# Norm's root and reciprocal on partitions, and one plain tile fewer in each feed-forward of a hybrid layer

## The chip, the cores and the metric

The kernel runs on 1 core of one Trainium2 chip. The metric is the device time of one execution in microseconds (us). A core has TensorE (PE, with its weight loads shown apart as PEld), VectorE (DVE), ScalarE (ACT), GpSimd (POOL) and SyncE (SP, which here only issues DMAs). Each engine takes its own instructions in order.

## The reference, cut to what matters

One transformer layer over 512 tokens with width 1024, all in fp32, with a feed-forward at either end:

```python
h = h + 0.5 * swiglu(rmsnorm(h, ffn1_norm), ffn1_w1, ffn1_w3, ffn1_w2)    # feed-forward a, D_FF = 2816
u = rmsnorm(h, mix_norm)
z = u @ w_in                       # q, k, v, gates of two attentions (NSA and MoBA)
h = h + (sigmoid(gate_a) * y_nsa + sigmoid(gate_b) * y_moba) @ w_out
h = h + 0.5 * swiglu(rmsnorm(h, ffn2_norm), ffn2_w1, ffn2_w3, ffn2_w2)    # feed-forward b
h = h + sigmoid(rmsnorm(h, ple_norm) @ w_ple_gate) * (p @ w_ple)
out = rmsnorm(h, final_norm)
# rmsnorm(x, g) = x * rsqrt(mean(x*x) + 1e-6) * g ;  swiglu = (silu(x@w1) * (x@w3)) @ w2
```

The row factor `rsqrt(...)` of a norm belongs to a token, so it can be multiplied in after a product with a weight matrix. The change concerns the row factors of three norms (those before feed-forward a, before the mixing stage, and before feed-forward b) and the two feed-forwards.

## The kernel before

Activations stand transposed: features on the 128 partitions, the 512 tokens in the free dimension. Each fp32 operand of a product is split in a high and a low part of a faster type, and a product is three matmuls, high by high, high by low, low by high (`mm3`, L226 to L229). A weight unit of 128x1024 arrives by DMA (`raw`), its high part is made on ACT (L76, in places POOL), its low part on DVE (L77); both stand in `whl`, of which there are three buffers.

**The norm's row factor.** `norm_rows` (L215) is called three times: for "a" and "b" inside `ffn_seven`, for "m" at L833, ahead of the mixing stage. `ssum` holds the squares summed over the 8 feature tiles. One fp32 matmul with a matrix of ones (L218) sums over the partitions and leaves each token's sum on all 128 partitions; ACT takes the root of the 128x512 (L220), DVE its reciprocal (L221). The result `R` has each token's factor on every partition. The norm ahead of the last stage (L1079 to L1084) is done in another way already: four matmuls with the tokens as output partitions and two columns of ones, a root and a reciprocal of 128x8.

**The feed-forward** (`ffn_seven`, L236) works through 22 tiles of 128 hidden features. The first `PLAIN` of them (6 in a, 5 in b) are *plain* tiles (L416 to L438): 24 matmuls of 512 columns for w1, 24 for w3. Their results are scaled by `R` and gated in `gate` (L253): two multiplications by `R`, one product, one low part on DVE; a silu and a high part on ACT. The others are *seven* tiles (L446 to L502): a tile's w1 and w3 are cut in quarters so that seven half-size products do for eight, 84 matmuls of 256 columns (`prod`, L346). These need other operands, the *forms*: `normal` (L295) multiplies `h` by gain and `R`, 8 instructions on DVE; `forms` (L298), 4 calls, makes sums and differences and splits them, 8 DVE and 4 ACT instructions each. Normals and forms are queued in `todo` and handed out one entry for each plain tile once `R` exists (L432). So the plain tiles are the time in which `R`, the normals, the forms and the first seven tile's weights (`wa`, `s2h`, `wb`) get ready. From the last plain tile on, each tile's result `gf` stays in fp32 until `convert` (L371) splits it at the end of the tiles; feature tile d of the down projection (L515 to L523) then runs over all 22 tiles in order.

**Order of the work.** Outside `tc.manual_schedule()` blocks a planner orders each engine's instructions ahead of time: earlier in the source means more urgent, but an instruction whose inputs the planner does not expect to be ready yet is passed by a later one. Inside those blocks (the seven tiles and the converts) the order is the source's. `tc.issue_after` keeps `norm_rows` in a feed-forward behind the w1 matmuls. PSUM has 8 banks by tag: "mm" 2, "s" 3, "t" 2, "po" 1. `p1` of a plain tile takes an "mm" bank, so tile f + 2 waits for `gate` of tile f. The sum `nb` takes a "t" bank, and so does the product `vcmp` right behind the norm "m" (L834).

Of the kernel before, what the change touches and what calls it, by code (L numbers as in the profile page):

```python
# [8 lines left out]
F32 = mybir.dt.float32  # L9
F32R = mybir.dt.float32r  # L10
AF = mybir.ActivationFunctionType
# [4 lines left out]
P = 128  # L16
S = 512
D = 1024
# [3 lines left out]
BIG = 1e30  # L22
EPS = 1e-6
NC_BLK = 31
PLAIN = {"a": 6, "b": 5}


class Weights:
# [87 lines left out]
def tile_hybrid_layer(ctx: ExitStack, tc: tile.TileContext, io, out):  # L116
    nc = tc.nc
    PSUM = bass.MemoryType.PSUM
    act, dve, pool, pe = nc.scalar, nc.vector, nc.gpsimd, nc.tensor

    def sbuf(stack, name, bufs=1):
        return stack.enter_context(tc.tile_pool(name=name, bufs=bufs, reuse_waits="tile"))
# [4 lines left out]
    nrm = sbuf(ctx, "nrm", 2)  # L127
# [4 lines left out]
    def bank(tag, name):  # L132
        return ps.tile([P, 512], F32, tag=tag, name=name, bufs={"s": 3, "po": 1}.get(tag, 2))
# [3 lines left out]
    for f in range(NF):  # L137
        units += [(("w1a", f), io["w1a"][f])]
        if f < PLAIN["a"]:
            units += [(("w3a", f), io["w3a"][f])]  # L140
# [17 lines left out]
    for f in range(NF):  # L158
        units += [(("w1b", f), io["w1b"][f])]
        if f < PLAIN["b"]:  # L160
            units += [(("w3b", f), io["w3b"][f])]
# [24 lines left out]
    ident = cst.tile([P, P], F32, name="ident")  # L186
    make_identity(nc, ident)
    ones = cst.tile([P, P], F32, name="ones")
    pool.memset(ones, 1.0)
    eps = cst.tile([P, 1], F32, name="eps")  # L190
# [3 lines left out]
    ssum, last_part = [None], [None]  # L194
# [20 lines left out]
    def norm_rows(n):  # L215

        b = bank("t", f"nb{n}")
        pe.matmul(b, lhsT=ones, rhs=ssum[0], start=True, stop=True)  # L218
        r = nrm.tile([P, S], F32, tag="R", bufs=1, name=f"R{n}")
        act.activation(r, b, AF.Sqrt, bias=eps, scale=1.0 / D)  # L220
        dve.reciprocal(r, r)  # L221
        return r

    last_mm = [None]
# [1 line left out]
    def mm3(out_ap, w, ah, al, first, last):  # L226
        pe.matmul(out_ap, lhsT=w[:, 0], rhs=ah, start=first, stop=False)  # L227
        pe.matmul(out_ap, lhsT=w[:, 0], rhs=al, start=False, stop=False)  # L228
        last_mm[0] = pe.matmul(out_ap, lhsT=w[:, 1], rhs=ah, start=False, stop=last)  # L229
# [5 lines left out]

    def ffn_seven(sfx, n, PLAIN, again, first=None):  # L236

# [15 lines left out]
        def gate(f, b1, b3):  # L253
            t1 = tp.tile([P, S], F32, tag="t1", name=f"t1{sfx}{f}")
            dve.tensor_mul(t1, b1, R)
            act.activation(t1, t1, AF.Silu)
            if f < PLAIN - 1:
                t3 = tp.tile([P, S], F32, tag="t3", name=f"t3{sfx}{f}")
            else:
                t3 = gf[f] = home(f)  # L260
            dve.tensor_mul(t3, b3, R)
            dve.tensor_mul(t3, t3, t1)
            if f < PLAIN - 1:
                ghl[f] = gp.tile([P, 2, S], F32R, tag=f"g{f}", name=f"g{sfx}{f}")
                parts(ghl[f], t3)

        def home(f):

            j = f - (PLAIN - 1)
            if j < 2 * KD:  # L270
# [24 lines left out]
        def normal(d):  # L295
            dve.scalar_tensor_tensor(h[d], h[d], gain[:, n - 1, d:d + 1], R, op0=ALU.mult, op1=ALU.mult)

        def forms(k):  # L298
            if not f11:
                form_tiles()  # L300
            a, b = h[k], h[k + 4]
            parts(f11[k], a[:, lo_])
            parts(f2[k], b)
            dve.tensor_sub(a[:, lo_], a[:, lo_], a[:, hi_])
            dve.tensor_sub(a[:, hi_], a[:, hi_], b[:, hi_])
            dve.scalar_tensor_tensor(b[:, hi_], a[:, lo_], -1.0, b[:, hi_], op0=ALU.mult, op1=ALU.subtract)
            dve.tensor_add(b[:, lo_], b[:, lo_], b[:, hi_])
            parts(f13[k], a)
            parts(f42[k], b)
# [4 lines left out]
        def load_sums(f):  # L314
            if f >= NF:
                return
            t = sums[f] = sp.tile([P, 2, Q], F32, tag="s13", name=f"s13{f}")
            nc.sync.dma_start(t[:, 0], w1[f][:, 0:Q])
            nc.sync.dma_start(t[:, 1], w3[f][:, Q:D])
            pool.dma_start(t, w3[f][:, 0:Q].unsqueeze(1).to_broadcast([P, 2, Q]), accum_op=ALU.add)  # L320

        def load_last(f):
            if f >= NF:
                return
            t = raws[f] = sp.tile([P, 2, Q], F32, tag="lr", name=f"lr{f}")
            nc.sync.dma_start(t[:, 1], w3[f][:, Q:D])
# [54 lines left out]
        def up_first(b1, b3):  # L381

            ws = [fp.tile([P, 2, 1024], F32R, tag=t, name=f"whl{u}") for u, t in enumerate(("fa", "fb0"))]
            odd = sp.tile([P, S], F32, tag="s2h", name="odd")
            ssum[0] = nrm.tile([P, S], F32, tag="ssum", bufs=1, name="ssum0")
            sqs = []
            with tc.manual_schedule():
                for k in range(KD):
                    if k % 2 == 0:
                        W.split_piece(0, k * P, k * P + 256, ws[0])  # L390
                    scaled(k, first, False)
                    if k % 2 == 0:
                        W.split_piece(1, k * P, k * P + 256, ws[1])
                    c = slice(k * P, (k + 1) * P)
                    for b, w in zip((b1, b3), ws):
                        mm3(b, w[:, :, c], uh[k], ul[k], k == 0, k == KD - 1)
                    if k % 2 == 0:
                        sq2 = sp.tile([P, 2, S], F32, tag=("s13", "lr")[k // 4], name=f"sq0_{k}")
                    act.activation(sq2[:, k % 2], h[k], AF.Square)
                    sqs.append(sq2[:, k % 2])  # L400
                    if k == 5:
                        pool.tensor_add(odd, sqs[1], sqs[3])
                act.activation(dummy, eps, AF.Sqrt)
                pool.tensor_add(odd, odd, sqs[5])
                pool.tensor_add(odd, odd, sqs[7])
                W.skip(2)
                for k in range(2, KD, 2):
                    dve.tensor_add(ssum[0], sqs[0] if k == 2 else ssum[0], sqs[k])
                W._split()
                dve.tensor_add(ssum[0], ssum[0], odd)  # L410
# [3 lines left out]
        todo = [lambda d=d: normal(d) for d in (0, 4, 1, 5, 2, 6, 3, 7)], *([lambda k=k: forms(k)] for k in range(4))  # L414
        todo = list(todo)
        for f in range(PLAIN):  # L416
            b1, b3 = bank("mm", f"p1{sfx}{f}"), bank("s", f"p3{sfx}{f}")
            if first is not None and f == 0:
                up_first(b1, b3)
            else:  # L420
                for b, key in ((b1, "w1"), (b3, "w3")):
                    w = W.get((key + sfx, f))
                    for k in range(KD):
                        c = slice(k * P, (k + 1) * P)
                        mm3(b, w[:, :, c], uh[k], ul[k], k == 0, k == KD - 1)
                    if R is None:
                        with tc.issue_after(last_mm[0].ins):
                            R = norm_rows(sfx)
            if last is not None:
                gate(*last)  # L430
            last = (f, b1, b3)
            if R is not None and todo:  # L432
                for x in todo.pop(0):
                    x()
            if f == PLAIN - 2:
                for x in range(2):
                    load_sums(PLAIN + x)
                    load_last(PLAIN + x)  # L438
# [76 lines left out]
        for d in range(KD):  # L515
            b = bank("t", f"p2{sfx}{d}")
# [7 lines left out]
        st.close()  # L524

    ffn_seven("a", 1, PLAIN["a"], io["xT"], 0)


# [100 lines left out]
    bias = [hp.tile([P, 4, 4, 32], F32, tag=f"h{6 + g}", name=f"bc{g}") for g in range(2)]  # L629
# [374 lines left out]
    def up_tile(w, e, o0, name):  # L1004
        b = bank("s" if o0 else "t", name)
        for k in range(4):
            c = slice((e * 4 + k) * P, (e * 4 + k + 1) * P)
            mm3(b, w[:, :, c], oh[o0 + k], ol[o0 + k], k == 0, k == 3)
        return b

    for d2 in range(4):
# [5 lines left out]
        for e in range(2):  # L1017
            d = 2 * d2 + e
            b = up_tile(w, e, 0, f"yn{d}")
            dve.tensor_mul(ga[d], b, ga[d])  # L1020
        w = W.get(("um", d2))
        for e in range(2):
            d = 2 * d2 + e
            b = up_tile(w, e, 4, f"ym{d}")
            t = gbq[d]
# [8 lines left out]
    for d in range(KD):  # L1034
        w = W.get(("wo", d))
        b = bank("mm", f"wo{d}")
        for k in range(KD):
            c = slice(k * P, (k + 1) * P)
# [29 lines left out]
    for i in range(4):  # L1068
        t = slice(i * P, (i + 1) * P)
        for e in range(2):  # L1070
            c = slice(e * 512, e * 512 + 512)
            b = bank("mm" if e else "s", f"pl{i}{e}")
# [12 lines left out]
    for i in range(4):  # L1085
        for e in range(2):
            b = bank("t" if e else "po", f"ht{i}{e}")
# [5 lines left out]
    for i in range(4):  # L1093
        t = slice(i * P, (i + 1) * P)
        ss, r = fin[:, i, 6:7], fin[:, i, 7:8]
        parts = [(0, 512), (512, 1024)] if i < 3 else [(0, 512), (512, 768), (768, 1024)]
        for e, (c0, c1) in enumerate(parts):
            c, n = slice(c0, c1), c1 - c0
            b = bank("mm" if e % 2 else "s", f"pg{i}{e}")[:, :n]
# [82 lines left out]
```

## Time and profile before

| | |
|---|---|
| median of 3 runs | 1193.08 us (1192.45 to 1193.95) |
| the profiled execution: time, span of its instructions | 1193.96 us, 1192.2 us |
| granted TensorE clock over the span | 0.999 of 2.4 GHz |
| PE busy | 1172.8 us (98%), 6714 matmuls |
| PEld busy | 1020.3 us (86%) |
| DVE busy | 796.3 us (67%) |
| ACT busy | 547.8 us (46%) |
| POOL busy | 192.9 us (16%) |

The span runs from the first to the last instruction; 1.8 us of the execution lie around it. Matmuls are pipelined: a row's own duration contains the flow through the array, so the cost of one matmul in a stream is the distance from its start to the next one's start.

### The profile page before, as it was taken

How to read it: one execution, taken by the hardware profiler on the slowest of the kernel's cores; microseconds unless marked ns; L12 is line 12 of the kernel's file. 1: busy time of each engine (PE TensorE's matmuls, PEld its weight loads, DVE VectorE, ACT ScalarE, POOL GpSimd, SP SyncE). 2: the span in 40 equal slices, each digit the busy share in tenths (PEclk: the TensorE clock that was granted, in tenths of full speed). 3: DMA queues.
4: the chain of work that ended last, by engine and by line, in shares of the span. 5: the costliest groups of instructions: out<-in, count | busy, mean ns of one | idle time of the engine just before them, and what ended most of it. 6: DMA issues, size and time to landing. Idle time of an engine off the chain costs nothing.

```text
span 1192.2 us, 17522 instructions
## 1 busy us (share of the span) xinstructions
PE 1172.8 (98%) x6714; PEld 1020.3 (86%) x6714; DVE 796.3 (67%) x1304; ACT 547.8 (46%) x920; POOL 192.9 (16%) x261
## 2 busy tenths in 40 slices
PE   8999999999999999999999999999999999999997
PEld 5889999988887878888888888888999999888876
DVE  6987777763336787776776655578777777533454
ACT  5544444542224564554457223354444445322355
POOL 3001111010025244333432100000111110100000
PEclk9999999999999999999999999999999999999999
DMA  7537777353333521212221343463677772533411
GB/s 240 156 90 187 185 179 185 102 197 113 116 109 110 164 71 36 72 36 78 82 89 54 124 137 124 140 182 106 151 182 177 191 183 80 183 97 97 155 56 53
DMA packets 57459, 151.09 MB, mean 127 GB/s; under 512 B 6256, under 2 KB 7408, under 8 KB 57376
## 3 DMA queue, kind: packets, MB, share of 16 engines
q1 hardware_dynamic: 41616, 116.77, 30.5%
q0 software_dynamic: 11584, 25.86, 11.4%
q10 hardware_dynamic: 4176, 7.36, 1.7%
q8 instruction: 52, 0.85, 0.3%
q14 instruction: 31, 0.25, 0.1%
HBM read 140.53 MB, written 6.29 MB: 123 GB/s over the span
## 4 chain that ended last, share of the span: by engine, by line
PE 87%; DVE 5%; issue 3%; POOL 2%; ACT 1%; DMA 1%; SPq 0%; ACTq 0%; POOLq 0%; DVEq 0%
PE pbb L351 6%; PE pba L351 6%; PE pab L351 4%; PE pdb L351 4%; PE paa L351 4%; PE pda L351 4%; PE p2b L227 3%; PE p2a L228 3%; PE p2a L229 3%; PE p2b L228 3%; PE p2b L229 3%; PE p2a L227 3%; DVE whl L77 2%; PE wo L228 1%; PE wo L227 1%
## 5 line engine op out<-in xcount | busy, mean ns | idle before, releaser
L77 DVE TENSOR_TENSOR whl<-raw,whl 128x1024 fp32r<-128x1024 f32 (+2 forms) x137 | 163.7, 1198 | 137.8 <-ACT whl L76 128.4
L76 ACT ACTIVATE whl<-raw 128x1024 fp32r<-128x1024 f32 (+2 forms) x105 | 106.5, 1019 | 238.2 <-issue 72.6
L341 DVE TENSOR_TENSOR wa<-raw,wa 128x1024 fp32r<-128x1024 f32 x33 | 40.4, 1225 | 63.1 <-ACT wa L338 63.1
L320 POOL DMA_DIRECT2D s<-in_w3b x17 | 20.6, 1210 | 254.3 <-DVE ssum L213 75.2
L74 POOL TENSOR_SCALAR whl<-raw 128x1024 fp32r<-128x1024 f32 x32 | 35.6, 1112 | 110.6 <-PE gb L229 29.8
L320 POOL DMA_DIRECT2D s<-in_w3a x16 | 19.5, 1218 | 177.7 <-DVE s L330 64.8
L341 DVE TENSOR_TENSOR wl<-lr,wl 128x1024 fp32r<-128x1024 f32 x33 | 40.1, 1216 | 4.1 <-ACT wl L338 4.1
L338 ACT ACTIVATE wb<-s 128x1024 fp32r<-128x1024 f32 x33 | 35.0, 1060 | 13.1 <-PE pbb L351 5.7
L341 DVE TENSOR_TENSOR wb<-s,wb 128x1024 fp32r<-128x1024 f32 x33 | 40.2, 1218 | 0.0
L362 ACT ACTIVATE c<-c 128x256 f32<-128x256 f32 x33 | 13.8, 418 | 57.4 <-DVE c L361 57.4
L228 PE MATMUL m<-ul,whl 128*128 128x512 f32 x96 | 37.8, 393 | 0.0
L229 PE MATMUL m<-uh,whl 128*128 128x512 f32 x96 | 37.7, 393 | 0.0
L227 PE MATMUL m<-uh,whl 128*128 128x512 f32 x96 | 37.6, 391 | 0.0
L338 ACT ACTIVATE wl<-lr 128x1024 fp32r<-128x1024 f32 x33 | 35.0, 1060 | 3.7
L338 ACT ACTIVATE wa<-raw 128x1024 fp32r<-128x1024 f32 x33 | 34.7, 1052 | 0.2 <-PE p3a L229 0.2
L351 PE MATMUL pbb<-fd,s2h 128*128 128x256 f32 x204 | 27.5, 284 | 0.2 <-DVE s2h L334 0.2
L351 PE MATMUL pab<-fc,wa 128*128 128x256 f32 x204 | 27.4, 284 | 0.0
L351 PE MATMUL pbb<-fc,wl 128*128 128x256 f32 x204 | 27.3, 283 | 0.0
L351 PE MATMUL pdb<-fd,wl 128*128 128x256 f32 x204 | 27.3, 283 | 0.0
L351 PE MATMUL pdb<-fb,wb 128*128 128x256 f32 x204 | 27.3, 283 | 0.0
L351 PE MATMUL pbb<-fb,wb 128*128 128x256 f32 x204 | 27.3, 283 | 0.0
L351 PE MATMUL pab<-f,wa 128*128 128x256 f32 x204 | 27.3, 283 | 0.0
(968 smaller groups left out, 3568.0 us busy)
## 6 DMA issues: line engine op xcount, KB each, us to landing
raw<-in_win SPq DMA_DIRECT2D x38, 512.0 KB, 3.7
raw<-in_w1b SPq DMA_DIRECT2D x22, 512.0 KB, 4.7
raw<-in_w1a SPq DMA_DIRECT2D x21, 512.0 KB, 4.8
s<-in_w3b POOLq DMA_DIRECT2D x17, 512.0 KB, 5.7
s<-in_w3a POOLq DMA_DIRECT2D x16, 512.0 KB, 5.8
raw<-in_w2a SPq DMA_DIRECT2D x16, 512.0 KB, 3.5
raw<-in_w2b SPq DMA_DIRECT2D x16, 512.0 KB, 3.6
s<-in_w1b SPq DMA_DIRECT2D x17, 256.0 KB, 3.2
```

The costliest lines, as they stand in the source:

```text
L74: nc.gpsimd.tensor_scalar(hi, src, 1.0, 0.0, op0=ALU.mult, op1=ALU.add)
L76: nc.scalar.activation(hi, src, AF.Copy)
L77: nc.vector.tensor_sub(lo, src, hi.bitcast(F32))
L227: pe.matmul(out_ap, lhsT=w[:, 0], rhs=ah, start=first, stop=False)
L228: pe.matmul(out_ap, lhsT=w[:, 0], rhs=al, start=False, stop=False)
L229: last_mm[0] = pe.matmul(out_ap, lhsT=w[:, 1], rhs=ah, start=False, stop=last)
L320: pool.dma_start(t, w3[f][:, 0:Q].unsqueeze(1).to_broadcast([P, 2, Q]), accum_op=ALU.add)
L338: act.activation(t[:, 0], src, AF.Copy)
L341: dve.tensor_sub(t[:, 1], src, t[:, 0].bitcast(F32))
L351: pe.matmul(b, lhsT=w[:, wz, c], rhs=fm(k, z), start=(first and k == 0 and wz + z == 0), stop=(k == 3 and wz == 1), skip_group_check=not f ...
L362: act.activation(c1[f][:, hi_], c1[f][:, hi_], AF.Silu)
```

## The change

`norm_rows` sums with the tokens on output partitions, as the last norm does: four fp32 matmuls with `ssum` as weights and two columns of ones. Root and reciprocal are taken of 128x8. Four TensorE transposes of a broadcast column spread the factors over the partitions again, into a second "t" bank, and ACT copies them to `R`. `PLAIN` falls from 6 to 5 and from 5 to 4, so 17 and 18 tiles are seven tiles instead of 16 and 17. The first plain tile after `R` takes two entries of `todo`, the normals and the first forms, so that all are still handed out.

```diff
-PLAIN = {"a": 6, "b": 5}
+PLAIN = {"a": 5, "b": 4}
...
     def norm_rows(n):

         b = bank("t", f"nb{n}")
-        pe.matmul(b, lhsT=ones, rhs=ssum[0], start=True, stop=True)
+        for i in range(4):
+            pe.matmul(b[:, 2 * i:2 * i + 2], lhsT=ssum[0][:, i * P:(i + 1) * P], rhs=ones[:, 0:2], start=True, stop=True)
+        c = nrm.tile([P, 8], F32, tag="rc", bufs=1, name=f"rc{n}")
+        act.activation(c, b[:, 0:8], AF.Sqrt, bias=eps, scale=1.0 / D)
+        dve.reciprocal(c, c)
+        rb = bank("t", f"rb{n}")
+        for i in range(4):
+            pe.transpose(rb[:, i * P:(i + 1) * P], c[:, 2 * i:2 * i + 1].to_broadcast([P, P]), ident)
         r = nrm.tile([P, S], F32, tag="R", bufs=1, name=f"R{n}")
-        act.activation(r, b, AF.Sqrt, bias=eps, scale=1.0 / D)
-        dve.reciprocal(r, r)
+        act.activation(r, rb, AF.Copy)
         return r
...
-            if R is not None and todo:
+            while R is not None and len(todo) >= PLAIN - f:
                 for x in todo.pop(0):
                     x()
```

## Rows read from the trace of the kernel before

**Rows 1.** The page's first part: busy time of each engine, its share of the span, and instructions.

```profile
PE 1172.8 (98%) x6714; PEld 1020.3 (86%) x6714; DVE 796.3 (67%) x1304; ACT 547.8 (46%) x920; POOL 192.9 (16%) x261
```

**Rows 2.** Busy time of each engine in stretches of the span: the plain tiles of a after its row factor, and the start of the mixing stage. Columns: stretch, its length, then busy us (instructions) of PE, PEld, DVE, ACT, POOL; granted clock, DMA share, GB/s.

```profile
42.00:76.00 34.00, 34.00 (x152) 28.17 (x151) 33.13 (x59) 16.75 (x24) 0.00 (x0) 1.00 0.35 107
372.00:388.00 16.00, 14.54 (x70) 11.40 (x69) 9.58 (x10) 6.86 (x9) 15.11 (x15) 1.00 0.32 96
```

**Rows 3.** What PE waited for, over the whole span: us in total, times, longest.

```profile
PE vB L227 <- DVE n01l L786: 1.6, 1, 1.6
```

**Rows 4.** PE in order of time, the first w1 matmul of the plain tiles 3 and 4 of a. Columns: start, us, engine, line, output and inputs, shapes, count.

```profile
43.78 0.39 PE L227 MATMUL p1a<-uh,whl 128*128 128x512 f32 x1
...
54.66 0.39 PE L227 MATMUL p1a<-uh,whl 128*128 128x512 f32 x1
```

**Rows 5.** PE in order of time, the first product of the seven tiles 6, 8 and 21 of a (12 matmuls each), and the second product of the first seven tile of b.

```profile
76.42 1.60 PE L351 MATMUL paa<-f,wa 128*128 128x256 f32 x12
...
94.36 1.60 PE L351 MATMUL paa<-f,wa 128*128 128x256 f32 x12
...
225.40 1.60 PE L351 MATMUL paa<-f,wa 128*128 128x256 f32 x12
...
833.29 1.60 PE L351 MATMUL pbb<-fd,s2h 128*128 128x256 f32 x12
```

**Rows 6.** PE in order of time, the norm's sum over the partitions in a (with the second matmul behind it), m and b.

```profile
26.39 1.02 PE L218 MATMUL nba<-ssum,ones 128*128 128x512 f32 x2
...
27.48 0.40 PE L228 MATMUL p3a<-ul,whl 128*128 128x512 f32 x1
...
363.51 1.02 PE L218 MATMUL nbm<-ssum,ones 128*128 128x512 f32 x2
...
782.00 1.02 PE L218 MATMUL nbb<-ssum,ones 128*128 128x512 f32 x2
```

**Rows 7.** PE in order of time, the last stage: the sum of the last norm (L1081), transposes (L1089) and the gate's matmuls (L1102 to L1104). In the source all transposes stand ahead of the gate's matmuls.

```profile
1134.51 0.95 PE L1081 MATMUL nbl<-ones,ssum 128*128 128x2 f32 x8
1135.32 1.07 PE L1089 MATMUL ht<-ident,hq 128*128 128x128 f32 x8
1136.14 0.48 PE L1102 MATMUL pg<-whl,uh 128*128 128x512 f32 x1
...
1138.43 0.66 PE L1089 MATMUL ht<-ident,hq 128*128 128x128 f32 x4 [1.57 <-DVE hn L1090]
1138.84 0.47 PE L1104 MATMUL pg<-whl,ul 128*128 128x512 f32 x1
1139.15 0.40 PE L1102 MATMUL pg<-whl,uh 128*128 128x512 f32 x1
```

**Rows 8.** Single instructions by line (duration in ns, min/median/max; first and last start): the root and the reciprocal of 128x8 and the table loads ahead of the roots of m and b; then, from ACT in order of time, a copy of 128x512 out of PSUM.

```profile
L1083 ACT ACTIVATE rn<-nbl,eps x1: 267/267/267, 1138.3 to 1138.3; 128x8 f32<-128x8 f32 x1
L1084 DVE RECIPROCAL rn<-rn x1: 193/193/193, 1139.7 to 1139.7; 128x8 f32<-128x8 f32 x1
L220 ACT ACT_TABLE_LOAD  x2: 1283/1283/1283, 364.8 to 783.3; - x2
1138.46 0.58 ACT L1090 COPY hn<-ht 128x512 f32<-128x512 f32 x1
```

**Rows 9.** ACT and DVE in order of time: root and reciprocal of a, and the first instruction that uses the row factor in a, m and b.

```profile
27.55 0.67 ACT L220 ACTIVATE Ra<-nba,eps 128x512 f32<-128x512 f32 x1
28.82 3.35 DVE L221 RECIPROCAL Ra<-Ra 128x512 f32<-128x512 f32 x1
32.20 0.69 DVE L255 TENSOR_TENSOR t1a<-p1a,Ra 128x512 f32<-128x512 f32 x1
...
370.24 0.69 DVE L644 TENSOR_TENSOR cf<-kcmp,Rm 128x512 f32<-128x512 f32 x1
...
788.67 5.39 DVE L296 SCALAR_TENSOR_TENSOR hr<-hr,gain,Rb 128x512 f32<-128x512 f32 x8
```

**Rows 10.** DVE in order of time, in the plain tiles of a and b: two low parts of weights, the first multiplication of the gate of tile 1, and the low parts of the first seven tile's weights.

```profile
39.91 2.35 DVE L77 TENSOR_TENSOR whl<-raw,whl 128x1024 fp32r<-128x1024 f32 x2
42.19 0.68 DVE L255 TENSOR_TENSOR t1a<-p1a,Ra 128x512 f32<-128x512 f32 x1
...
73.62 0.68 DVE L334 TENSOR_TENSOR s2h<-s,s2h 128x512 fp32r<-128x512 f32 x1
74.22 1.22 DVE L341 TENSOR_TENSOR wb<-s,wb 128x1024 fp32r<-128x1024 f32 x1
...
827.88 0.68 DVE L334 TENSOR_TENSOR s2h<-s,s2h 128x512 fp32r<-128x512 f32 x1
```

**Rows 11.** The down projection of b: its first matmul and the low-part matmul of tile 13 on PE, and the converts of tiles 13 to 16 on DVE.

```profile
1003.88 0.40 PE L227 MATMUL p2b<-gb,whl 128*128 128x512 f32 x1
...
1012.98 0.42 PE L228 MATMUL p2b<-gbfc,whl 128*128 128x512 f32 x1
...
1012.15 2.50 DVE L251 TENSOR_TENSOR gbfc<-gfb,gbfc 128x512 fp32r<-128x512 f32 x4
```

**Rows 12.** The start of the mixing stage: POOL's sums for the compression inputs, the scaling of the second query tile on DVE, and the matmul that waits for its bank on PE.

```profile
371.01 16.93 POOL L653 TENSOR_TENSOR xa<-cf,pos 64x248 f32<-64x248 f32 x16 [4.78 <-DVE cf L644]
386.78 0.68 DVE L559 SCALAR_TENSOR_TENSOR q1f<-q,Rm 128x512 f32<-128x512 f32 x1
387.60 0.47 PE L227 MATMUL kA<-uh,whl 128*128 128x512 f32 x1 [1.46 <-DVE q1f L559]
```

## The prediction

> **What bounds the kernel now.** I read the page's busy times first: PE is busy for 98% of the span, DVE for 67% [rows 1], so the time is PE's instruction stream and the few places where that stream stops. Then the list of PE's waits, which is short; the one that lies behind the norms and could move is 1.6 us for `vB` [rows 3], and a second one shows in PE's order of time, 1.46 us ahead of `kA` [rows 12]. Last the stretches: in the plain tiles of a PE never stops, but DVE is busy for 33.1 of 34.0 us beside it [rows 2]. So PE is the bound and DVE is just below it there. A change can gain by making PE's stream shorter or by removing a wait; a plain tile dropped takes 10.9 us of cover away from DVE.
>
> **The tile that changes its kind.** A plain tile lasts 54.66 - 43.78 = 10.88 us on PE, 48 matmuls at 0.227 us [rows 4]. Thirteen seven tiles last 225.40 - 94.36 = 131.04 us, 10.08 us each, 84 matmuls at 0.120 us [rows 5]. One tile in each feed-forward: 2 x (10.08 - 10.88) = **-1.60 us**.
>
> The Trainium skill (TensorE: Matmul & The Clock Gate, section Back-to-back issue gap) puts the gap between matmuls at the columns over 2.4 GHz plus 2.5 ns, so 216 ns and 109 ns here; a plain tile would take 10.4 us, a seven tile 9.2 us, and the term would be -2.4 us. Both distances in this trace are longer (227 and 120 ns), the short one by more, so the sum keeps the rows' -1.60.
>
> **The norm on PE, three times.** Before: the sum starts at 26.39, the second matmul behind it at 27.48, so the first would start at 27.25 in a plain stream: 0.86 us [rows 6]. After: eight passes of the two-column form, 1135.32 - 1134.51 = 0.81 us; four transposes, 1138.84 - 1138.43 = 0.41 us; and after each block the next 512-column matmul costs about 0.09 more than 0.227 (behind the transposes 1139.15 - 1138.84 = 0.31) [rows 7]. That is 0.81 + 0.41 + 2 x 0.09 = 1.40, or +0.54 each, **+1.62 us** for three. So on PE alone the two halves of the change cancel. The stationary operand is a broadcast column, which no row shows; it has 128 columns as the shown transposes have, so I take their price.
>
> **When R is there.** Removed from the chain: a root of 128x512 and a reciprocal of 3.35 us on DVE [rows 9]. Added: root 0.27, reciprocal 0.19, copy 0.58 [rows 8], transposes 0.66 to their end [rows 7], and two more handovers between engines, estimated at 0.1 each. In m and b the chain behind the table load goes from 0.69 + 3.35 to 1.90 us: R comes about 2.1 us earlier, near 368.1 instead of 370.24 and near 786.6 instead of 788.67 [rows 9]. The table load of 1.28 us stays in both [rows 8]. In a the reciprocal could start at 28.82 as now, since DVE is in a low part until then; 3.35 - 0.19 - 0.66 - 0.58 - 0.3 leaves 1.6 us, so the first use moves from 32.20 to about 30.6.
>
> **Whether DVE still finishes in time.** Between the first use of R and the low part of `s2h`, DVE works without a gap. One tile fewer removes four gate instructions at a distance of 0.60 and two low parts of weights at 1.14 (42.19 - 39.91 is 2.28 for two) [rows 10]: 4.68 us. In a `s2h` is ready at 74.22 now, then at 74.22 - 1.6 - 4.68 = 67.9. PE needs it in the third matmul of the second product: first seven tile at 76.42 - 10.88 + 0.54 = 66.1, one product of 1.44 and two matmuls later, 67.8 [rows 5, 10]. That is 0.2 us late. The second place is the gate of tile 1, which frees the bank for `p1` of tile 3: the first forms now stand ahead of it, five half-size and three full-size DVE instructions, estimated from the 0.60 at 3.5 us. So it ends at 42.19 - 1.6 + 3.5 + 0.7 = 44.8 against a need at 43.78 + 0.54 = 44.3 [rows 4, 10]. Late by 0.5; what PE waits here it need not wait at `s2h`, so a costs **+0.5 us** (bounds: 0, if the planner puts the gate first, and 1.6, if none of R's gain reaches DVE). In b `s2h` moves from 828.5 to 828.5 - 2.1 - 4.68 = 821.7 and is needed at 833.29 - 10.88 + 0.54 + 0.24 = 823.2 [rows 5, 10]: 1.5 us to spare, nothing.
>
> **The down projection.** It runs over the tiles in order, 0.68 us each, while the converts are still being made in a written order. In b the first convert of the group that starts at 1012.15 ends near 1012.84, and PE's low-part matmul of tile 13 starts at 1012.98, so 0.14 us is to spare [rows 11]. With one tile more to convert, the same place in that order holds tile 12, needed 0.68 earlier: **+0.54 us** in b. In a the order comes to stand as it stands in b now, where PE does not stop: nothing.
>
> **The mixing stage.** Ahead of `kA` PE waits 1.46 us for a bank that `q1f` empties at 386.78, after a chain that starts with POOL's 17 us of sums behind R [rows 12]. All of it moves 2.1 us earlier, while PE is 0.54 later, so the wait goes: **-1.46 us**. Bounds: 0, if DVE's order puts other work ahead of `q1f`; no more than 1.46.
>
> **Waits that the change adds.** The transposes wait for root and reciprocal, and behind them in PE's queue stand the matmuls of the same tile. The last stage shows that the planner lets later matmuls pass transposes that are not ready: the source has all transposes first, but gate matmuls run at 1136.14 and 1138.84 between them [rows 7]. It shows too that it can be wrong by 1.57 us. Bounds: 0, and the whole chain, worked out below as a rival. Between them I take 0.1 each, **+0.3 us**. Each added seven tile brings its own loads, one of them issued and summed through POOL's queue, in place of a plain tile's two; POOL is busy for 16% [rows 1] and the order of the loads stays. ACT gets a copy of 0.58 for a root of 0.67. Nothing for these.
>
> **The sum:** -1.60 + 1.62 + 0.5 + 0.54 - 1.46 + 0.3 = -0.1 us. It is made against the profiled execution's 1193.96 us (span 1192.2 and 1.8 around it), which lies 0.9 above the median of 1193.08. On the median: **1193.0 us**.
>
> **The rivals.**
> *The transposes stop PE (slower).* If the planner puts them right behind the sum, PE waits for the whole chain. The sum ends 0.95 after its start; in m at 364.5, in b at 783.0 [rows 6, 7], table load, root and reciprocal end near 366.7 and 785.1 [rows 8]: 2.2 us each; in a about 1.8. Together 6.2 instead of 0.3: 1198.9 us. In m the bank of `vcmp` does the same, if both "t" banks are given to the norm first. It decides from 2.8 us in all three. The mixed order in rows 7 speaks against, the 1.57 us there for. Chance 0.14.
> *Every cover holds and the wait at `vB` goes too (faster).* -1.60 + 1.62 - 1.46 - 1.63 = -3.1: 1190.0 us. The planner orders the attention anew, and R's users lie ahead of that wait; but its releaser is a small DVE instruction far from R [rows 3]. Chance 0.14.
> *R comes no earlier*, because splits of weights go ahead of the chain on ACT and DVE, while 10.9 us of cover are gone: a is then late by 1.8 and b by 0.6 instead of 0.5 and 0: 1194.9 us, with `kA`'s wait back 1196.3. That would be the change not doing what it says. In a, ACT takes the root 0.2 after the sum [rows 6, 9], so little stands ahead of it. Chance 0.07.
> *`kA` still waits* because DVE's order keeps `q1f` late: 1194.5 us. Chance 0.12.
> *The transposes run one after the other*, each for the 0.27 us of its row and not for the distance of 0.10: 4 x 0.27 - 0.41 = 0.67 more in each norm, 1195.0 us. Four in 0.66 us to the last one's end speak against it [rows 7]. Chance 0.04. The Trainium skill (TensorE: Matmul & The Clock Gate, section Part 4: PE-mode transpose) gives about 275 ns for a transpose within a kernel; by that rule this rival would be the forecast. The trace agrees with the duration, not with a stream of that distance.
>
> **How the numbers follow.** The forecast as summed has 0.49; its own range is the new plan's chance of shifting waits by about 1.4 us either way, 1191.6 to 1194.4. The 8-in-10 range goes on toward the faster rival and over the last three: 1190.5 to 1195.8; outside it stay most of the first two rivals' far ends. A measurement of this kernel can tell about 0.2% (2.4 us) from no change. Faster than 1190.7: the faster rival and 0.01, 0.15. Slower than 1195.5: the first rival and about half of the third, 0.17. The rest, 0.68, is within.
>
> **What would show each step.** In the trace after: a seven tile still 10.08 apart; about 1.4 us of PE per norm; first uses of R near 30.6, 368, 786.5; no wait at `kA`; a wait of about 0.5 at `p1a` of tile 3 or `s2h`; about 0.5 in the down projection of b behind a `gbfc` convert; none there in a. The prediction is wrong if the transposes show waits of 1 us or more, if DVE is over 1 us late at the first seven tile, or if the attention's waits, re-planned, change by more than 2 us in sum.

## The result, and the profile after

| | us, median (lowest to highest, runs) | profiled execution | span | mean granted clock |
|---|---|---|---|---|
| before | 1193.20 (1192.45 to 1193.95, 4) | 1193.96 | 1192.2 | 0.999 |
| after | 1200.26 (1199.78 to 1201.27, 4) | 1200.47 | 1198.8 | 0.998 |

The ratio is 1.0058, with a 95% interval of 1.0046 to 1.0069: slower by 7 us, where 1193.0 was forecast and 1195.8 was the upper end. Of one kernel below (128 bytes and `h6`) two slow executions, 1275.53 and 2341.08 us, are left out of its median. First the busy times of the changed kernel, to be read against [rows 1]:

```profile
PE 1181.1 (99%) x6816; PEld 1025.8 (86%) x6816; DVE 794.7 (66%) x1318; ACT 554.1 (46%) x931; POOL 195.2 (16%) x263
```

PE has 102 instructions more, as the change has it: 10 in each of three norms (eight passes and four transposes for two passes) and 36 in each of two tiles (84 matmuls for 48). But it is busy for 8.3 us more, and the sum priced these 102 at 0.02 us. Then PE's waits over the whole span (us in total, times, longest):

```profile
PE p1a L234 <- DVE ul L202: 2.1, 3, 1.4
PE vB L233 <- DVE n01l L792: 1.6, 1, 1.6
PE pba L357 <- ACT s2h L338: 1.4, 1, 1.4
...
PE pba L357 <- DVE s2h L340: 0.9, 2, 0.6
...
PE p2b L234 <- DVE gbfc L257: 0.3, 1, 0.3
```

The wait of `kA` [rows 12] is gone, the one of `vB` [rows 3] is as it was, and feed-forward a has new ones, for `s2h`, of 2.1 us at its first seven tile. So one part of the loss is a wait, and a larger part lies in time in which PE counts as busy. Where, one sees by cutting the span at the first instruction of each stage, by PE's order of time. The last column is a repaired kernel that the experiments below lead to. (The first row, the start, differs by a us between executions that do the same work there: it is 25.69 in the kernel with all moved by 32 bytes and 26.64 in the one with 512 unused bytes.)

| from the first instruction of ... to that of ... | before | after | difference | repaired |
|---|---|---|---|---|
| start to `nba` | 26.39 | 27.21 | +0.82 | 25.79 |
| `nba` to `paa` (plain tiles of a) | 50.03 | 40.51 | -9.52 | 39.53 |
| `paa` to `p2a` (seven tiles of a) | 161.93 | 174.68 | +12.75 | 172.09 |
| `p2a` to `kcmp` (down projection) | 119.71 | 119.74 | +0.03 | 119.74 |
| `kcmp` to `nbm` | 5.45 | 5.60 | +0.15 | 5.45 |
| `nbm` to `kA` | 24.09 | 23.38 | -0.71 | 23.04 |
| `kA` to `yn` | 266.62 | 267.84 | +1.22 | 266.75 |
| `yn` to `p1b` | 122.31 | 123.17 | +0.86 | 122.30 |
| `p1b` to `nbb` | 5.47 | 5.59 | +0.12 | 5.46 |
| `nbb` to `pab` (plain tiles of b) | 49.86 | 40.51 | -9.35 | 39.51 |
| `pab` to `p2b` (seven tiles of b) | 172.02 | 182.04 | +10.02 | 182.04 |
| `p2b` to `nbl` | 130.63 | 131.36 | +0.73 | 131.31 |
| `nbl` to the end | 57.69 | 57.17 | -0.52 | 56.19 |

Two things are out of line. The seven tiles of a grow by 12.75 us, where those of b grow by 10.02, one tile. And stretches that the change does not touch are longer by small amounts. The shortest of these is the plainest: 24 matmuls of 512 columns, from the first of `p1b` to the sum of the norm, with no wait between them. The view is PE in order of time; first the kernel before, whose sum starts at 782.00 [rows 6], then the changed one.

```profile
776.53 0.39 PE L227 MATMUL p1b<-uh,whl 128*128 128x512 f32 x1
```

```profile
782.13 0.40 PE L233 MATMUL p1b<-uh,whl 128*128 128x512 f32 x1
...
787.72 0.95 PE L219 MATMUL nbb<-ones,ssum 128*128 128x2 f32 x8
```

5.47 / 24 = 0.228 us before, 5.59 / 24 = 0.233 after: the same matmul on the same operands, with a longer step from one start to the next. Over the whole trace (mean step between neighbouring starts within one tile, worked out from the start times, without steps over 1.2 times the median) it is so wherever `uh`, `ul` meet the split weights `whl`: `kcmp` 226.7 to 233.3 ns, the last gate `pg` 226.9 to 233.4, the gates `gb` 228.1 to 233.0. The output logits `pl` keep 226.6 and 226.8, the down projections 226.7 to 227.0; the up projections and `wo` have 233.2 to 233.5 in both. Each difference of means times its count is in sum some 6.7 us.

The second thing, in a: PE around its first seven tile, and beside it DVE.

```profile
67.72 1.60 PE L357 MATMUL paa<-f,wa 128*128 128x256 f32 x12
70.74 0.51 PE L357 MATMUL pba<-fd,s2h 128*128 128x256 f32 x2 [1.43 <-ACT s2h L338]
71.88 1.46 PE L357 MATMUL pba<-fd,s2h 128*128 128x256 f32 x10 [0.64 <-DVE s2h L340]
...
68.14 0.68 DVE L257 TENSOR_TENSOR fd<-h,fd 128x512 fp32r<-128x512 f32 x1
68.74 0.68 DVE L267 TENSOR_TENSOR gfa<-p3a,Ra 128x512 f32<-128x512 f32 x1
69.34 0.68 DVE L336 TENSOR_TENSOR s<-s,raw 128x512 f32<-128x512 f32 x1
...
71.14 0.68 DVE L340 TENSOR_TENSOR s2h<-s,s2h 128x512 fp32r<-128x512 f32 x1
```

The sum `s`, the first step of the second product's weights, stands behind `fd`, the last of the forms. Its tile's name explains it: it takes the buffer `h{6 + f % 2}` by the tile's number f. With the first seven tile at 6 that was `h6`; at 5 it is `h7`, one of the eight tiles of the activations, which the last forms read. So it cannot be written before the last form has been made.

### The profile page after: what moved, and what is told of

The parts are those of the page before. It is cut to its first block, busy times and chain, and to the rows that moved or that the text cites. A ratio compares the mean times of both kernels' runs of the same rounds, so it can differ in the third digit from the quotient of the medians.

```text
span 1198.8 us, 17774 instructions
## 1 busy us (share of the span) xinstructions
PE 1181.1 (99%) x6816; PEld 1025.8 (86%) x6816; DVE 794.7 (66%) x1318; ACT 554.1 (46%) x931; POOL 195.2 (16%) x263
## 4 chain that ended last, share of the span: by engine, by line
PE 90%; DVE 5%; ACT 2%; issue 2%; POOL 1%; DMA 0%; SPq 0%; ACTq 0%; POOLq 0%; DVEq 0%
PE pbb L357 6%; PE pba L357 6%; PE pab L357 4%; PE pdb L357 4%; PE pda L357 4%; PE paa L357 4%; PE p2a L234 3%; PE p2a L233 3%; PE p2a L235 3%; PE p2b L234 3%; PE p2b L235 3%; PE p2b L233 3%; PE m L233 2%; PE m L234 2%; PE m L235 2%
## 5 line engine op out<-in xcount | busy, mean ns | idle before, releaser
L77 DVE TENSOR_TENSOR whl<-raw,whl 128x1024 fp32r<-128x1024 f32 x133 | 158.5, 1194 | 136.7 <-ACT whl L76 127.0
L76 ACT ACTIVATE whl<-raw 128x1024 fp32r<-128x1024 f32 (+2 forms) x101 | 102.4, 1018 | 227.4 <-issue 68.3
L347 DVE TENSOR_TENSOR wa<-raw,wa 128x1024 fp32r<-128x1024 f32 x35 | 42.9, 1224 | 67.2 <-ACT wa L344 65.2
L347 DVE TENSOR_TENSOR wl<-lr,wl 128x1024 fp32r<-128x1024 f32 x35 | 42.6, 1216 | 4.1 <-ACT wl L344 4.1
L347 DVE TENSOR_TENSOR wb<-s,wb 128x1024 fp32r<-128x1024 f32 x35 | 42.6, 1218 | 0.0
L357 PE MATMUL pba<-fd,s2h 128*128 128x256 f32 x204 | 27.9, 285 | 2.3 <-ACT s2h L338 1.4
```

Of the source, the lines that this page charges most:

```text
L76: nc.scalar.activation(hi, src, AF.Copy)
L77: nc.vector.tensor_sub(lo, src, hi.bitcast(F32))
L347: dve.tensor_sub(t[:, 1], src, t[:, 0].bitcast(F32))
L357: pe.matmul(b, lhsT=w[:, wz, c], rhs=fm(k, z), start=(first and k == 0 and wz + z == 0), stop=(k == 3 and wz == 1), skip_group_check=not f ...
```

## The experiments

Each was timed 5 to 11 times beside the kernel before, which had medians of 1193.07 to 1193.23 in these groups. The theory after the comparison: (A) the 32-byte tile `rc`, put into a pool that lies between the activations and the split weights, moves everything behind it by 32 bytes, and the matmuls are slower for it; (B) the buffer `h7` makes the wait in a. The rival to A is that something the new norm does slows the matmuls; to B, that DVE is late in any order, as the prediction had feared.

**Which address counts.** A pool is a stretch of the on-chip memory that a group of tiles shares; pools lie one behind the other, and every address here is a byte within a partition. In the compiled program of before, `uh` starts at byte 34112 of a partition and `whl` at 87360, 53248 = 208 x 256 later.

*32 unused bytes in the kernel before, between the two:*

```
     nrm = sbuf(ctx, "nrm", 2)
...
+    spare = nrm.tile([P, 8], F32, tag="spare", bufs=1, name="spare")
+    pool.memset(spare, 0.0)
```

> The kernel before, with one unused tile of 32 bytes on each partition in the pool ahead of the weights, written once by POOL at the start; no other change, so norm, tiles and order are those of before. Theory A: 512-column matmuls of plain tiles, projections and last gate go from 0.227 to 0.2333 us and the time rises by 6 to 7 us, to about 1199.7. Theory B: 1193.2 us, distances of 0.227.

Measured: 1198.82 us, ratio 1.0051 (1.0039 to 1.0063). Nothing is computed with these bytes. PE in order of time:

```profile
780.27 0.40 PE L229 MATMUL p1b<-uh,whl 128*128 128x512 f32 x1
...
785.87 0.59 PE L220 MATMUL nbb<-ssum,ones 128*128 128x512 f32 x1
```

5.60 us for the same 24 matmuls. The rival to A falls: unused bytes alone, without any of the change, cost 5.6 us.

*The same 32 bytes in the first pool (`cst` for `nrm`), so that all moves together:*

> The kernel before, with the same unused 32 bytes, but in the first pool, so that activations and weights move by the same amount. Tells two forms of theory A apart. If the distance of the weights from the activations counts: no change, 1193.2 us and 0.227. If a weight tile's own address counts: as slow as with the weights alone moved, about 1199.7 us. Theory B: 1193.2 us.

Measured: 1192.97, ratio 1.0002 (0.9993 to 1.0011), 5.46 us for the 24:

```profile
775.88 0.39 PE L229 MATMUL p1b<-uh,whl 128*128 128x512 f32 x1
...
781.34 1.02 PE L220 MATMUL nbb<-ssum,ones 128*128 128x512 f32 x2
```

So what counts is not where an operand lies but how far the two lie apart.

*The tile of the changed kernel made 128 bytes instead of 32:*

```
-        c = nrm.tile([P, 8], F32, tag="rc", bufs=1, name=f"rc{n}")
+        c = nrm.tile([P, 32], F32, tag="rc", bufs=1, name=f"rc{n}")[:, 0:8]
```

> The changed kernel, with the new 128x8 tile of the norm (32 bytes on each partition) enlarged to 128 bytes; nothing else. The trace of the changed kernel shows 512-column matmuls of the feed-forwards' plain tiles, the mixing stage's projections and the last gate at 0.2333 us from start to start, against 0.227 before; the down projections stay at 0.227. Theory A (place in memory): the 32 bytes move every tile that is allocated behind them, the split weights among them, against the activations uh and ul in front of them, and a matmul pays for that. Then the distances return to 0.227 and the time falls by about 6.7 us (the sum over tile names of the count times the difference), to 1193.6 us. Theory B (order): the matmuls are slower because of what DVE and ACT do beside them in the new order, or the loss lies in waits; then nothing changes, 1200.3 us.

Measured: 1200.62, ratio 1.0064 (1.0052 to 1.0076), steps near 232.4 ns. This did not bring the time back, as theory A had expected with this distance; a distance that is a multiple of 128 is not enough. So the next two went on, with spare tiles in the kernel before as above:

*512 unused bytes:*

> The kernel before with an unused tile of 512 bytes between the activations and the split weights, so that their distance goes from 53248 (26 times 2048) to 53760. If the pitch depends on the distance modulo 512 or less, the matmuls stay at 0.227 and the time at 1193; if on it modulo 1024 or 2048, they go to 0.233 and the time to 1198.8, as with 32 bytes.

*256 unused bytes:*

> The kernel before with an unused tile of 256 bytes between activations and split weights (distance 53504). 32 bytes cost 5.6 us and 128 bytes left the pitch at 0.2324, while 512 bytes cost nothing. If the period is 256 bytes the pitch stays 0.227 and the time 1193.2; if it is 512, the pitch is 0.232 to 0.233 and the time 1198 to 1199.

Measured: 1193.10, ratio 1.0000 (0.9991 to 1.0009), and 1193.32, ratio 1.0001 (0.9992 to 1.0010). Both are as before.

*The other way round: operands that were badly placed in the kernel before.* `oh`, `ol`, `mh`, `ml` lie 51904 bytes behind `whl`, 192 more than a multiple of 256.

```
     dn = ExitStack()
+    pad = sbuf(dn, "dpad").tile([P, 336], F32, name="dpad")
+    pool.memset(pad, 0.0)
     dp = sbuf(dn, "dn")
```

> The kernel before with 1344 unused bytes ahead of the operands of the two up projections and the mixing output (the tiles oh, ol, mh, ml), which brings their distance to the split weights from 51904 to 53248 bytes, a multiple of 2048. The theory that the distance sets the pitch: the 384 matmuls of yn, ym and wo, at 0.2333 us in the kernel before, go to 0.2267, worth 384 x 0.0066 = 2.5 us: 1190.7. Rival (these matmuls are slow for another reason, such as their waits or the weights of their pieces): no change, 1193.2.

Measured: 1190.89, ratio 0.9981 (0.9972 to 0.9990). PE in order of time, the first `wo` matmul and the first of `p1b`, 192 matmuls later; first the padded kernel, then the one before, where `p1b` starts at 776.53:

```profile
730.57 0.39 PE L227 MATMUL wo<-mh,whl 128*128 128x512 f32 x1
...
774.09 0.39 PE L227 MATMUL p1b<-uh,whl 128*128 128x512 f32 x1
```

```profile
731.73 0.39 PE L227 MATMUL wo<-mh,whl 128*128 128x512 f32 x1
```

43.52 / 192 = 0.2267 against 44.80 / 192 = 0.2333. The same rule, at another place, with the activations above the weights in memory instead of below them. In one table (distance in bytes between activations and split weights, the rest that it leaves when divided by 256, and the step from one start to the next):

| kernel | distance | rest | us per matmul |
|---|---|---|---|
| before, and moved together | 53248 | 0 | 0.228, 5.47 and 5.46 / 24 |
| 32 spare, and after | 53280 | 32 | 0.233, 5.60 and 5.59 / 24 |
| after with 128 | 53376 | 128 | 0.2325, 5.58 / 24 |
| 256 spare | 53504 | 0 | 0.2275, 5.46 / 24 |
| 512 spare | 53760 | 0 | 0.228, 5.47 / 24 |
| before, `wo` | 51904 | 192 | 0.2333, 44.80 / 192 |
| padded, `wo` | 53248 | 0 | 0.2267, 43.52 / 192 |

**The buffer.** *The changed kernel with 128 bytes, and the second product's weights in the buffer they had:*

```
-            t = hp.tile([P, Q], F32, tag=f"h{6 + f % 2}", name=f"s2{f}")
+            t = hp.tile([P, Q], F32, tag=f"h{6 + (f - PLAIN) % 2}", name=f"s2{f}")
```

> The enlarged-tile version, and the tile in which the first seven tile's s2 is summed takes the buffer h6 instead of h7 in feed-forward a (the two alternate by tile number, now counted from the first seven tile; in b this gives h6 as the number itself does with 4 plain tiles). In the changed kernel PE stops 2.1 us at the first s2h of a and 0.2 at the second, and s2's sum starts on DVE right behind the last low part that reads h7, the last of the forms. Theory C (buffer): the sum waits for h7, which only the last forms release; with h6, released one call earlier, the wait falls below 0.7 us and the time by 1.4 to 2 us against the enlarged-tile version, to about 1192 us. Theory D (DVE is simply full, as the prediction had it): no more than 0.3 us better, 1193.5 us.

Measured: 1196.29, ratio 1.0027 (1.0016 to 1.0038). The 1192 of the expectation counted on 128 bytes to bring the steps back to 0.227, which they did not. The wait goes, as B says, but the gain on 1200.62 is 4.3 us where the waits were 2.1. The next pair shows why.

*The changed kernel with its tile in the first pool, so at the distance of before:*

```
-        c = nrm.tile([P, 8], F32, tag="rc", bufs=1, name=f"rc{n}")
+        c = cst.tile([P, 8], F32, tag="rc", name=f"rc{n}")
```

> The changed kernel with its 32-byte tile of sums taken from the first pool of SBUF, ahead of the activations, in place of the pool that lies between the activations and the split weights: so activations and weights keep the distance that they had before (53248 bytes) and only everything together lies 32 bytes on. Theory A (the distance between the two operands sets the pitch of the matmuls): the 512-column matmuls of the feed-forwards, the mixing projections and the output product go back from 0.233 to 0.227 us, and the time falls by 6 to 7 us, to 1193.5 to 1194.5. Rival (something in the new norm itself slows the matmuls, or the sum of the stalls is the cause): the pitch stays 0.233 and the time 1200. What is left over the kernel before is then the late buffer of feed-forward a's second product (1.4 to 2 us at its first two row blocks).

*The same with the buffer of before (both edits), the repaired kernel of the table above:*

> The same, and the tile of the second scale and shift takes the buffer that the kernel before used for it (h6 in feed-forward a, h7 in b), so that it no longer waits for the last tile's forms. Theory: the waits for s2h in feed-forward a (1.4 and 0.6 us) go, the pitch is 0.227, and what is left of the change is what it was priced at: a tile of 0.80 us fewer in each feed-forward, three norms that start earlier and cost 0.5 us more on PE, no wait of kA: 1190 to 1192. Rival: the earlier norm and the one tile fewer are worth nothing, since the work that they free ends in a wait further on (vB, the forms of the last tiles): 1193.

Measured: 1196.02, ratio 1.0022 (1.0014 to 1.0031), and 1191.45, ratio 0.9984 (0.9976 to 0.9993). The step goes back to 0.227 in both, and the second is what the change is worth without the two side effects. Its second edit acts in a alone: in b the changed kernel's numbering gives `h6` already, where the kernel before had `h7` (not the buffer of before, as the expectation has it). DVE of the second in a; the sum now stands ahead of the last form `fd`:

```profile
63.27 0.68 DVE L336 TENSOR_TENSOR s<-s,raw 128x512 f32<-128x512 f32 x1
...
65.75 0.68 DVE L340 TENSOR_TENSOR s2h<-s,s2h 128x512 fp32r<-128x512 f32 x1
66.35 0.68 DVE L257 TENSOR_TENSOR fd<-h,fd 128x512 fp32r<-128x512 f32 x1
```

The first came out above its expectation. PE in order of time at its first seven tile:

```profile
65.68 1.59 PE L357 MATMUL paa<-f,wa 128*128 128x256 f32 x12
69.23 0.80 PE L357 MATMUL pba<-fd,s2h 128*128 128x256 f32 x2 [1.96 <-ACT s2h L338]
70.37 2.50 PE L357 MATMUL pba<-fd,s2h 128*128 128x256 f32 x10 [0.35 <-DVE s2h L340]
72.67 2.76 PE L357 MATMUL paa<-fc,wa 128*128 128x256 f32 x12
75.23 1.94 PE L357 MATMUL pda<-fb,wb 128*128 128x256 f32 x12
77.01 1.60 PE L357 MATMUL pba<-fb,wb 128*128 128x256 f32 x12
```

The twelve `paa` matmuls at 72.67 take 2.56 us to the next group, 0.213 each, where 0.120 is the rule [rows 5]. The wait itself is 2.3 us; the seven tiles of a last 177.36 us here and 172.09 in the repaired kernel, 5.3 more. The granted clock by stretches (columns as in [rows 2]) says what the other 3 us are; the rows are, one kernel each, of this kernel, of the changed kernel and of the one with 128 bytes:

```profile
66.00:72.00 6.00, 3.69 (x20) 3.20 (x19) 4.32 (x7) 1.25 (x3) 0.00 (x0) 0.77 0.36 103
72.00:78.00 6.00, 6.00 (x38) 6.00 (x37) 1.53 (x2) 1.33 (x2) 1.20 (x1) 0.66 0.58 140
```

```profile
70.00:75.00 5.00, 3.62 (x28) 3.42 (x29) 2.25 (x5) 0.75 (x2) 0.42 (x1) 1.00 0.66 206
```

```profile
70.00:75.00 5.00, 4.17 (x23) 3.97 (x24) 1.70 (x4) 0.13 (x1) 0.79 (x1) 0.74 0.68 210
```

The stalled engine fell to the clock's lower level, 1.2 GHz, and worked there until near 76. The profiled execution of the changed kernel had a pause of 2.1 us and kept its clock; with 128 bytes, waits of 1.5 and 0.6 us and the clock fell. The Trainium skill (TensorE: Matmul & The Clock Gate, section What's actually happening) knows two levels only, half and full, and says of the rise to full speed at a kernel's start that its moment differs from run to run. By the half level 256 columns are an estimate of 256 / 1.2 GHz = 0.213 us, which the trace agrees with. In the seven tiles of a the pauses of 2.1 to 2.3 us cost 2.6 us where the clock stayed (174.68 against 172.09), and 4.0 (128 bytes, 176.04) and 5.3 where it fell. The executions of the kernel with its tile in the first pool spread over 1193.67 to 1197.80, which would fit a clock that fell in some of them only; a trace was kept of one.

The four kernels together (medians): h7 at a bad distance 1200.3 (128 bytes: 1200.6), h6 at a bad distance (128 bytes) 1196.3, h7 at a good one 1196.0, h6 at a good one 1191.45. The distance is worth 4.2 to 4.8 us, the buffer 4.3 to 4.6. That the distance is worth less here than the 5.6 us of 32 bytes in the kernel before is only in part accounted for: with 128 bytes the step is a little shorter than with 32, and with `h7` the kernel at the good distance lost clock in its profiled execution while the changed one did not.

**The two halves of the change apart.** *One tile fewer alone* (`PLAIN` of 5 and 4, the loop over the forms as in the change, the old norm; the buffer `h6`, which is that of before in a):

> One part of the change alone: one plain tile fewer in each feed-forward, with the norm as it was, and the second product's tile in the buffer that it had before (so without the wait for the last forms). No tile is added, so the distance between activations and weights is that of before. Theory: the two tiles give 2 x 0.80 = 1.6 us; against it stands the first use of the factor of the norm, which without the new norm comes some 1.1 us (feed-forward a) and 1.5 us (b) later in relation to the last plain tile than in the changed kernel, so that DVE, which has no slack left there, is late at the second product's first operand by up to that much: 1191.6 to 1194.2, taken 1192.5. Rival: DVE isn't late, the tiles come in full: 1191.6. Other rival: DVE is so late that PE pauses for over 2 us and the granted clock falls as in the kernel with the tile in the first pool: 1196 or more.

Measured: 1194.37, ratio 1.0011 (1.0002 to 1.0020). PE in order of time at the first seven tile of a:

```profile
65.38 1.59 PE L351 MATMUL paa<-f,wa 128*128 128x256 f32 x12
67.97 0.50 PE L351 MATMUL pba<-fd,s2h 128*128 128x256 f32 x2 [0.99 <-ACT s2h L332]
69.27 1.46 PE L351 MATMUL pba<-fd,s2h 128*128 128x256 f32 x10 [0.80 <-DVE s2h L334]
```

DVE is late by 1.8 us although the buffer is the right one, and the seven tiles of a grow by 12.47 us instead of 10.08. In b nothing waits there: plain and seven tiles together give 0.73 us back. The time is just above what was expected (taken 1192.5, bounds to 1194.2): the lateness in a is 1.8 us and not the 1.1 by which the factor is later.

*The new norm alone* (its tile in the first pool, six and five plain tiles):

> The other part alone: the new norm, with its 32-byte tile in the first pool so that the distance to the weights stays, and six and five plain tiles as before. Theory by the measured stretches: the norm costs PE 0.4 to 0.5 us more at each of its three places in the layer, +1.3 to +1.6; the wait of kA (1.46) and the one at the last stage (1.6) go; feed-forward tiles don't gain from the earlier factor: 1191.5 to 1193.2, taken 1192.3. Rival: the waits come back elsewhere and the norm costs its PE time in full: 1194.8.

Measured: 1192.70, ratio 0.9995 (0.9986 to 1.0004): as expected, and not clear of no change. Its stretches: `nba` to `paa` +0.36, `nbm` to `kA` -1.03, `nbb` to `pab` +0.53.

So the halves need each other: +1.3 and -0.4 apart, -1.8 together. The earlier factor is what lets DVE finish with one tile less of cover; with six tiles it is worth nothing in a.

**All repairs together.** *The repaired kernel with the 1344 bytes ahead of the up projections' operands:*

> The changed kernel with the tile of sums in the first pool, the buffer of the second product as before, and 1344 unused bytes ahead of the operands of the up projections and the mixing output. If the three effects add, 1191.45 - 2.4 = 1189.0, faster than both kernels (0.9965). If the 2.4 us of the last are partly a wait's, 1190.

Measured: 1189.21, ratio 0.9965 (0.9952 to 0.9977): the effects add, and it is faster than both kernels.

## Why the prediction was wrong, step by step

**The step that failed first** is not in the sum at all. "A seven tile still 10.08 apart", the plain tiles' 0.227 and every other time from start to start were carried over from [rows 4, 5], because the change does not touch those instructions. It touches their operands' places: a tile of 32 bytes in a pool in front of the weights. The prediction thus put at nothing, without a look at the addresses, a term of 5.6 us, as the 32 unused bytes show.

**The second** is the place of `s2h` in a. The prediction worked out when DVE would be free for it, "0.2 us late", and did not ask which buffer it takes and who reads that last. The term was 0.5 us, with bounds of 0 and 1.6; the changed kernel waits 2.1, past the prediction's own sign of being wrong ("over 1 us late at the first seven tile"). The repaired kernel makes its `s2h` at 65.75 and PE does not stop at it; the changed one makes it at 71.14. In the seven tiles of a that is 2.6 us in the changed kernel's profile (174.68 - 172.09); the pairs of kernels that differ in the buffer alone have 4.3 and 4.6 in their medians, and in both the profiled execution with `h7` lost clock behind the wait.

**The norm on PE**, +0.54 each: right in size, a little high. PE in order of time, in b (the sum starts at 787.72 above):

```profile
791.64 0.60 PE L225 MATMUL rbb<-ident,rcb 128*128 128x128 f32 x4
791.99 0.48 PE L234 MATMUL p3b<-ul,whl 128*128 128x512 f32 x1
792.30 0.39 PE L235 MATMUL p3b<-uh,whl 128*128 128x512 f32 x1
```

Four transposes in 0.35 us and 0.08 behind them; the sum takes 0.81 in a (27.21 to 28.02). Together about 1.32 for 0.86, or +0.46. No wait stands at any of the transposes, so the rival of the stopped PE and the one of serial transposes fall, and the 0.3 us for their waits is nothing.

**The tile**: right. In b, -10.35 + 10.02 = -0.33, which is -0.80 and the norm's 0.46.

**When R is there**: too early by 0.5. ACT and DVE in order of time, in m:

```profile
370.36 0.27 ACT L221 ACTIVATE rcm<-nbm,eps 128x8 f32<-128x8 f32 x1
372.21 0.60 ACT L227 ACTIVATE Rm<-rbm 128x512 f32<-128x512 f32 x1 [1.58 <-PE rbm L225]
...
370.66 0.20 DVE L222 RECIPROCAL rcm<-rcm 128x8 f32<-128x8 f32 x1 [0.36 <-ACT rcm L221]
372.85 0.69 DVE L650 TENSOR_TENSOR cf<-kcmp,Rm 128x512 f32<-128x512 f32 x1 [1.98 <-ACT Rm L227]
```

```profile
371.58 0.60 PE L225 MATMUL rbm<-ident,rcm 128*128 128x128 f32 x4
```

From root to first use 2.49 us, estimated 1.90. The reciprocal ends at 370.86 and the transposes start at 371.58: PE is not stopped for them, but in its queue they stand behind gate matmuls, which run until then. From the norm's sum to the first use of R it is 5.11 us in m for 6.73 [rows 6, 9], 5.18 in b for 6.67, 4.71 in a for 5.81: 1.6, 1.5 and 1.1 earlier, where 2.1, 2.1 and 1.6 were named.

**DVE late in a**, +0.5: nothing in the repaired kernel, whose first seven tile has no wait; the tile alone, without the earlier R, is late by 1.8. The rival "R comes no earlier" had put just that at 1.8 in a (and at 0.6 in b, where nothing waits).

**The down projection of b**, +0.54: right. `p2b` to `nbl` grows by 0.68 in the repaired kernel; the wait is where it was said to be, at a `gbfc` convert. PE in order of time in the changed kernel:

```profile
1019.28 0.50 PE L234 MATMUL p2b<-gbfc,whl 128*128 128x512 f32 x1 [0.26 <-DVE gbfc L257]
```

In a nothing, as said (119.71 and 119.74).

**The wait of `kA`**, -1.46: right. It is in no list of waits of a kernel with the new norm, and is in the one with the tile alone.

**The sum** was -0.1 and the repaired kernel gives -1.8 by medians. The 0.5 for DVE and the 0.3 for the transposes' waits did not come, which is about half of that. The last stage's wait for `ht` [rows 7] adds nothing that can be counted on: over the kernels with the old norm it is between nothing and 1.6 us, and the profiled execution of before happened to have the longest one, which may be why it lay 0.9 above the median. So the sum's own terms were too dear by 1.7 us together, and the loss came from the two places above.

## What to carry to other kernels

Before a change is priced by its instructions, list what it allocates: a new tile, however small, moves every pool behind it, and a buffer chosen by a number's parity changes its owner when the number moves. Put small tiles where no distance between matmul operands depends on them, and compare the mean step between untouched matmuls in both traces first; it settles at once whether a loss is everywhere or at one place. A pause of some 2 us on PE is to be priced with the slower clock that may follow it: 2.6 to 5.3 us here.

## What the hardware showed that was not expected

A 512-column matmul of the split fp32 operands follows its neighbour by 0.227 us where the distance between its two operands in a partition is a multiple of 256 bytes, and by 0.2325 to 0.2333 at rests of 32, 128 and 192, 3% more, in the feed-forwards and the mixing projections as in the up projections and `wo`. It is the same in the last gate `pg`, where the activations are the stationary operand and the weights stream. The place of both together does not matter (32 bytes more for all: 1.0002). Rests of 64 and others were not tried; why a multiple of 256 is good is not shown by these runs, and neither is whether it is the reading of the weights or of the activations that waits.

Narrower matmuls do not follow the rule. The last two parts of `pg` have 256 columns, 24 matmuls each. PE in order of time, the first of either part, in the kernel before (rest 0) and in the changed one (rest 32):

```profile
1178.99 0.28 PE L1102 MATMUL pg<-whl,uh 128*128 128x256 f32 x1
...
1181.87 0.28 PE L1102 MATMUL pg<-whl,uh 128*128 128x256 f32 x1
```

```profile
1185.47 0.28 PE L1108 MATMUL pg<-whl,uh 128*128 128x256 f32 x1
...
1188.27 0.28 PE L1108 MATMUL pg<-whl,uh 128*128 128x256 f32 x1
```

2.88 / 24 = 0.120 us before and 2.80 / 24 = 0.117 after: at this width the rest of 0 is the slower one (0.119 with 128 bytes). The seven tiles' products of 256 columns have 0.120 and rest 0 in every kernel here; whether another rest would make them faster was not tried.
